# Mixer in the order of the source, scores of two query blocks in two joined PSUM banks, turned five steps behind

## The chip, the core and the metric

The kernel runs on one core of one Trainium2 chip. The metric is the device time of one execution in microseconds; runs of one kernel agree within about 0.05% here (three runs between 880.33 and 881.12). Five engines work side by side: TensorE (PE; matmuls, with PEld for its weight loads), VectorE (DVE), ScalarE (ACT), GpSimd (POOL) and SyncE (SP), whose queue issues most DMA transfers. Each takes its own instructions in the order in which they were built, and waits on semaphores for the others.

## The reference

One layer of an encoder on 512 positions of 1024 features: half a SwiGLU feed-forward network, a mixer, the other half, a final norm.

```python
x = x + 0.5 * swiglu(rms_norm(x, ffn1_norm), ffn1_w_gate, ffn1_w_up, ffn1_w_down)
h = rms_norm(x, mix_norm)
u = h @ w_in                       # 512 Fourier | 8 x 64 q | 2 x 64 k | 2 x 64 v
f_out = fourier_mixer(u[..., :512])            # Re(DFT over positions and channels), a linear map per group
a_out = gqa_attention(q, k, v)                 # norm of q and k, axial rotary, softmax over all 512 keys
x = x + concatenate([f_out, a_out]) @ w_out
x = x + 0.5 * swiglu(rms_norm(x, ffn2_norm), ffn2_w_gate, ffn2_w_up, ffn2_w_down)
return rms_norm(x, final_norm)
```

## The kernel before

The activations lie transposed, features on the 128 partitions and 512 positions along the row: `x` is eight tiles of 128x512. Every product of float32 values is made of three matmuls (`product`, L100): each factor is split into a rounded high part (a cast, by ScalarE in L96 or VectorE in L94) and a low part (`lows`, L72, always VectorE), and high x high, high x low and low x high are added in PSUM. So each weight tile of 128x1024 costs a DMA into a raw tile (`raw_tile`, L85, three buffers, issued by SP), a cast and a `lows` before TensorE can use it. `ring` holds the split weights and the split input `hh`, `hl`; two more slots, `more`, are lent to the mixer.

The program has three stages: FFN1, the mixer, FFN2. The two FFN stages stand in `in_order()`: in them the instructions of TensorE and SP keep the order of the source. The mixer stands outside, so that the framework's scheduler orders all five engines there, by its own estimate of times. VectorE, ScalarE and GpSimd are ordered by that scheduler everywhere. One PSUM pool, `pp` (L51), of eight banks of 128x512 serves all stages; a tile gets a bank when the bank's earlier tile has been read.

The mixer first projects keys (`k`), the first query pair (`q0`) and values (`v`), each 24 matmuls; `rope` rotates keys and queries, and for q1 to q3 moves rows by four small DMAs from `own_q` to `sw_q`, issued by SP (L606). `heads` sums squares per head on TensorE (`pq`, eight columns), and `keys` and `value_stacks` prepare `kst` and `vst`. Four query tiles t = 0 to 3 hold two heads each (b = 0, 1), and each head has four blocks c of 128 queries: 32 steps. In step n `attend(n)` does

- `scores` (L786) of block n: two matmuls of 512 columns into a bank `s`, the negated maximum `mx` over 512 keys on VectorE (L796), its product with the scale (L797), the exponential `e` on ScalarE with its row sum (L799);
- `turn` (L802) of step n - 4: four transposes of `e` into a bank `pt`, a cast to `ph` (ScalarE, L808) and a low part `pl` (VectorE). A turn needs all four blocks of its head;
- `values` (L818) of step n - 6: two matmuls into a bank `o`, and after four of them the sum of its halves into `oo`; after both heads transposes of the row sums (`zp`), a product, and a split into `qa`, `qb`.

Between the steps a list `fill` (L873 to L906) is worked off in proportion: the projections of q1 to q3, then those of the Fourier group (`fproject`, 24 matmuls of 256 columns for a bank `f`, then `fu`, `fe`, `eh`, `el`), the folded map (`fold`), the transforms (`positions`, `dft` and `channels`, `pc`, `psn`, `fq`, `fo`). The raw weights of each come when its `load`, `fload` or `weights` call is made. At last eight `out` tiles (L929) take 24 matmuls each over the eight parts `mh`, `ml` (four Fourier groups, four query tiles), are added to `x`, and feed the norm of FFN2.

## Time and profile before

| | |
|---|---|
| runs | 880.33, 880.73, 881.12 us; median 880.73 |
| the profiled execution | 881.16 us, of which the span of its instructions is 879.4 us |
| granted TensorE clock | 0.996 of full speed |
| FFN1 / mixer / FFN2, by the first k and first gate matmul | to 353.2 us / to 523.5 us / to 879.4 us |
| scores of the 32 steps | 379.2 to 462 us |

A row of the timeline has start, duration, engine, line, operation, output<-inputs, shape and count; in brackets the idle time of the engine before it and what ended that. A matmul's row is longer than the distance to the next start, because matmuls are pipelined. Names of tiles are the program's, without numbers: all `s` banks are `s`. A row of the waits has who waited for whom, the total in us, how often, and the longest.

### The profile page before, as it was taken

To read this page: it belongs to the slowest core of one execution; us is meant where nothing else is said; L and a number is where in the kernel's file an instruction comes from. 1 tells how busy PE (TensorE), PEld (TensorE's weight loads), DVE (VectorE), ACT (ScalarE), POOL (GpSimd) and SP (SyncE) were. 2 spreads that over 40 slices of the span, in tenths; PEclk is the share of its full clock that TensorE was granted. 3 is DMA by queue.
4 is the path that set the end of the run, shared out by engine and by line. 5 is a ranking of instruction groups with operands and counts; after the bars stand their busy time and mean duration, and the time that the engine had idled before them with its cause. 6 is when DMAs were issued, how large, how long until landed. Compare 5 with 4: busy or idle time off the path is not lost.

```text
span 879.4 us, 13481 instructions
## 1 busy us (share of the span) xinstructions
PE 864.5 (98%) x5358; PEld 767.9 (87%) x5358; DVE 641.0 (73%) x1006; ACT 450.4 (51%) x746; POOL 22.9 (3%) x29
## 2 busy tenths in 40 slices
PE   8999999999999999999999999999999999999996
PEld 5888999889989988888888888879998999889986
DVE  7798788459757837699888558977975688459553
ACT  7454466326524635677775446535652366326441
POOL 0000000000000000211000000000000000000001
PEclk9999999999999999999999999999999999999998
DMA  7324232332243113521110213242323232322212
GB/s 247 111 70 164 97 116 85 99 116 105 69 141 114 56 37 108 204 84 37 50 48 25 87 68 133 76 140 98 108 79 129 84 120 82 101 115 86 73 37 96
DMA packets 29151, 85.57 MB, mean 97 GB/s; under 512 B 3488, under 2 KB 6560, under 8 KB 28960
## 3 DMA queue, kind: packets, MB, share of 16 engines
q1 hardware_dynamic: 28560, 83.37, 27.8%
q0 software_dynamic: 384, 1.32, 0.4%
q8 instruction: 42, 0.69, 0.3%
q14 instruction: 21, 0.17, 0.1%
q10 hardware_dynamic: 144, 0.02, 0.0%
HBM read 81.81 MB, written 2.10 MB: 95 GB/s over the span
## 4 chain that ended last, share of the span: by engine, by line
PE 56%; issue 38%; DVE 3%; ACT 2%; DMA 1%; POOL 0%; SPq 0%; DVEq 0%; ACTq 0%; POOLq 0%
PE r L319 10%; PE q L319 5%; PE dn L103 4%; PE dn L102 4%; PE dn L101 4%; PE p L319 3%; PE gu L103 2%; PE gu L102 2%; PE gu L101 2%; PE out L101 2%; PE out L103 2%; PE out L102 2%; PE pt L805 1%; PE q L101 1%; PE q L102 1%
## 5 line engine op out<-in xcount | busy, mean ns | idle before, releaser
L319 PE MATMUL r<-rt,ring 128*128 128x256 f32 x1584 | 207.0, 283 | 0.0
L319 PEld LDWEIGHTS r<-rt,ring 128*128 128x128 f32 x1584 | 196.0, 188 | 2.4
L101 PE MATMUL dn<-at,ring 128*128 128x512 f32 x318 | 125.7, 395 | 0.8 <-ACT ring L96 0.8
L103 PE MATMUL dn<-at,ring 128*128 128x512 f32 x318 | 125.8, 396 | 0.3 <-DVE ring L72 0.3
L102 PE MATMUL dn<-at,ring 128*128 128x512 f32 x318 | 125.6, 395 | 0.0
L405 DVE SCALAR_TENSOR_TENSOR xt<-dn,xt 128x512 f32<-128x512 f32 x61 | 42.1, 689 | 87.4 <-PE dn L103 87.3
L319 PE MATMUL q<-rt,ring 128*128 128x256 f32 x792 | 104.7, 281 | 0.0
L96 ACT CAST ring<-raw_dn 128x768 fp32r<-128x768 f32 (+3 forms) x64 | 48.1, 754 | 107.5 <-PE dn L102 89.1
L319 PEld LDWEIGHTS q<-rt,ring 128*128 128x128 f32 x792 | 98.7, 188 | 0.0
L72 DVE TENSOR_TENSOR ring<-s,ring 128x1024 fp32r<-128x1024 f32 x66 | 80.3, 1220 | 16.9 <-PE r L319 9.7
L280 ACT CAST ring<-s 128x1024 fp32r<-128x1024 f32 x66 | 69.3, 1051 | 37.5 <-PE r L319 19.2
L103 PEld LDWEIGHTS dn<-at,ring 128*128 128x128 f32 x318 | 59.8, 188 | 15.6 <-DVE ring L72 1.5
L101 PEld LDWEIGHTS dn<-at,ring 128*128 128x128 f32 x318 | 59.8, 188 | 14.9 <-ACT ring L96 1.3
L102 PEld LDWEIGHTS dn<-at,ring 128*128 128x128 f32 x318 | 59.8, 188 | 13.7
L72 DVE TENSOR_TENSOR ring<-raw_dn,ring 128x768 fp32r<-128x768 f32 (+3 forms) x64 | 54.5, 854 | 12.0 <-ACT ring L96 9.7
L319 PE MATMUL p<-rt,ring 128*128 128x256 f32 x396 | 52.4, 281 | 0.0
L72 DVE TENSOR_TENSOR ring<-raw_g,ring 128x1024 fp32r<-128x1024 f32 x33 | 40.3, 1223 | 15.4 <-PE p L319 10.9
L319 PEld LDWEIGHTS p<-rt,ring 128*128 128x128 f32 x396 | 49.3, 188 | 0.0
L280 ACT CAST ring<-raw_g 128x1024 fp32r<-128x1024 f32 x33 | 34.6, 1050 | 22.8 <-PE r L319 9.9
L101 PE MATMUL gu<-ring 128*128 128x512 f32 x112 | 44.5, 397 | 0.5 <-ACT ring L542 0.5
L102 PE MATMUL gu<-ring 128*128 128x512 f32 x112 | 44.1, 393 | 0.0
L103 PE MATMUL gu<-ring 128*128 128x512 f32 x104 | 41.0, 394 | 0.7 <-DVE ring L72 0.7
(312 smaller groups left out, 1531.3 us busy)
## 6 DMA issues: line engine op xcount, KB each, us to landing
raw_g<-in_wgu SPq DMA_DIRECT2D x33, 512.0 KB, 3.8
raw_u<-in_wgu SPq DMA_DIRECT2D x33, 512.0 KB, 4.2
raw_dn<-in_wd SPq DMA_DIRECT2D x40, 384.0 KB, 3.1
raw_gu<-in_wgu SPq DMA_DIRECT2D x16, 512.0 KB, 3.6
raw_o<-in_wo SPq DMA_DIRECT2D x8, 512.0 KB, 3.5
raw_in<-in_wins SPq DMA_DIRECT2D x6, 512.0 KB, 4.0
raw_dn<-in_wd SPq DMA_DIRECT2D x8, 320.0 KB, 2.9
raw_dn<-in_wd SPq DMA_DIRECT2D x8, 256.0 KB, 2.6
```

Source lines behind the costliest of these rows:

```text
L72: nc.vector.tensor_tensor(out=lo, in0=src, in1=asf(hi), op=ALU.subtract)
L96: nc.scalar.copy(hi[:, :n, :], raw[:, :n, :])
L101: nc.tensor.matmul(ps, whi, mhi, start=first, stop=False)
L102: nc.tensor.matmul(ps, whi, mlo, start=False, stop=False)
L103: nc.tensor.matmul(ps, wlo, mhi, start=False, stop=last)
L280: nc.scalar.copy(hi, src)
L319: nc.tensor.matmul(ps, a[:, ks], b[:, i], start=first and i == 0 and o == 0, stop=i == KH - 1 and o == 2, skip_group_check=not first,)
L405: nc.vector.scalar_tensor_tensor(out=x[d][:, t], in0=ps[:, t], scalar=0.5, in1=x[d][:, t], op0=ALU.mult, op1=ALU.add)
L805: nc.tensor.transpose(pt[:, c * P : (c + 1) * P], prob[t, b, c][:, kc * P : (kc + 1) * P], ident)
```

## The change

The mixer moves into `in_order()`, so TensorE's and SP's instructions keep the source's order there too. PSUM is no longer one pool: FFN1 has a pool of eight banks, the mixer one of six and a tile `st` of two joined banks, FFN2 again eight. `scores` now does two blocks at a time, in even steps: four matmuls into the halves of `st`, one maximum over both (128x2 from 128x2x512), one product, two exponentials. `st` is one tile, so each pair writes where the pair before stood. `turn` comes five steps after a step's number instead of four, `values` seven instead of six, and the loop has 39 steps.

The DMA for raw weights is separated from their split: `fetch` issues it at places written into the source, and `project` and `fload` take the raw tile. cos and sin come after the third weight tile. Some calls move by a few matmuls (`key_scales` after seven parts of q0 instead of five, `keys` after all of `v`, `value_stacks` after part five of q1). `out` sums its parts in the order 0, 1, 2, 4, 5, 6, 3, 7. Of all instructions only the maxima and their products change in number, from 32 each to 16.

In the built program two more waits stand: the first k matmul waits for VectorE's residual of FFN1's last `dn` bank, and the first gate matmul of FFN2 for the residual of the last `out` bank.

```diff
-    pp = ctx.enter_context(tc.tile_pool(name="psum", bufs=8, space=bass.MemoryType.PSUM))
+    pools = []
+
+    def banks_in(name, n):
+        return tc.tile_pool(name=name, bufs=n, space=bass.MemoryType.PSUM)

     def bank(name):
-        return pp.tile([P, S], F32, tag="bank", name=name)
+        return pools[-1].tile([P, S], F32, tag="bank", name=name)
...
-    with in_order():
+    with in_order(), banks_in("psum1", 8) as psum:
+        pools.append(psum)
+        warm()
         ffn(n0, n1, A["wgu1"], A["wd1"], A["wdt1"], GROUPS1, opening1, None)
...
-    with tc.tile_pool(name="mix", bufs=1) as mp, tc.tile_pool(name="mixt", bufs=1) as mt:
+    with (
+        in_order(),
+        tc.tile_pool(name="mix", bufs=1) as mp,
+        tc.tile_pool(name="mixt", bufs=1) as mt,
+        banks_in("psum2", 6) as psum,
+        banks_in("psum3", 1) as two,
+    ):
+        pools.append(psum)
...
+        st = two.tile([P, 2, S], F32, name="st")
+
+        def scores(t, b, c0):
+
+            if b == 0 and c0 == 0:
                 zs[t] = tp.tile([P, 4, 2], F32, tag="z", bufs=2, name=f"z{t}")
             q = (qa, qb)[b][t]
-            cs = slice(c * P, (c + 1) * P)
-            ps = bank(f"s{t}{b}{c}")
-            nc.tensor.matmul(ps, q[:, cs], kst[b][0], start=True, stop=False)
-            nc.tensor.matmul(ps, q[:, cs], kst[b][1], start=False, stop=True)
-            f = sc[:, c, 2 + 2 * t + b : 3 + 2 * t + b]
-            mx = tp.tile([P, 1], F32, tag="mx", bufs=8, name=f"mx{t}{b}{c}")
-            nc.vector.tensor_reduce(out=mx, in_=ps, axis=AX.X, op=ALU.max, negate=True)
-            nc.vector.tensor_tensor(out=mx, in0=mx, in1=f, op=ALU.mult)
-            e = temp(f"e{t}{b}{c}")
-            nc.scalar.activation(e, ps, AF.Exp, bias=mx, scale=f, accum_out=zs[t][:, c, b : b + 1])
-            prob[t, b, c] = e
+            both = range(c0, c0 + 2)
+            for c in both:
+                cs = slice(c * P, (c + 1) * P)
+                nc.tensor.matmul(st[:, c - c0], q[:, cs], kst[b][0], start=True, stop=False)
+                nc.tensor.matmul(st[:, c - c0], q[:, cs], kst[b][1], start=False, stop=True)
+            i = 2 + 2 * t + b
+            mx = tp.tile([P, 2], F32, tag="mx", bufs=4, name=f"mx{t}{b}{c0}")
+            nc.vector.tensor_reduce(out=mx, in_=st, axis=AX.X, op=ALU.max, negate=True)
+            nc.vector.tensor_tensor(out=mx, in0=mx, in1=sc[:, c0 : c0 + 2, i], op=ALU.mult)
+            for c in both:
+                e = temp(f"e{t}{b}{c}")
+                o = c - c0
+                nc.scalar.activation(
+                    e, st[:, o], AF.Exp, bias=mx[:, o : o + 1], scale=sc[:, c, i : i + 1],
+                    accum_out=zs[t][:, c, b : b + 1],
+                )
+                prob[t, b, c] = e
...
+        fetch(0)
+        fetch(1)
         key = project(0, "k")
         q0 = project(1, "q0")
+        fetch(5)
+        nc.sync.dma_start(out=cos, in_=A["cos"])
+        nc.sync.dma_start(out=sin, in_=A["sin"])
         run(key)
         rope("k", qkg[:, 1:2])
         n1.column([n1.acc])
+        fetch(2)
         val = project(5, "v")
-        run(q0[:5])
+        run(q0[:7])
         key_scales()
-        run(q0[5:])
+        run(q0[7:])
...
+                if k == 2:
+                    add(fetch, (4, "f0", "f1")[t - 1])
                 if t == 3 and k in (0, 4):
                     add(fload, k // 4)
-                if k == 3:
+                if t == 3 and k == 6:
+                    add(fetch, "f2")
+                if k == 5 if t == 1 else k == 3:
...
-            if n < 32:
+            if 5 <= n < 37:
+                turn(*at(n - 5))
+            if n < 32 and n % 2 == 0:
                 scores(*at(n))
-            if 4 <= n < 36:
-                turn(*at(n - 4))
-            if n >= 6:
-                values(*at(n - 6))
+            if n >= 7:
+                values(*at(n - 7))
...
+        ready = 0, 1, 2, 4, 5, 6, 3, 7
         for d in range(KD):
             whi, wlo = weights(A["wo"][d], f"o{d}")
             ps = bank(f"out{d}")
-            for k in range(KD):
-                product(ps, whi[:, k, :], wlo[:, k, :], mh[k], ml[k], k == 0, k == KD - 1)
+            for k in ready:
+                product(ps, whi[:, k, :], wlo[:, k, :], mh[k], ml[k], k == ready[0], k == ready[-1])
...
-    with in_order():
+    with in_order(), banks_in("psum4", 8) as psum:
+        pools.append(psum)
          ffn(n2, n3, A["wgu2"], A["wd2"], A["wdt2"], GROUPS2, lambda gate, column, row: [[gate(0, {KD - 1: column}), gate(1, {3: row})]], closing)
```

More of the change, by code (lines that the diff above doesn't have):

```diff
@@ L506, in encoder, with warm @@
     nc.vector.memset(idle, 0.0)
-    busy = bank("busy")
-    for _ in range(WARM):
-        nc.tensor.matmul(busy, idle[:, 0:P], idle, start=True, stop=True)
+    def warm():
+        busy = bank("busy")
+        for _ in range(WARM):
+            nc.tensor.matmul(busy, idle[:, 0:P], idle, start=True, stop=True)
     n0, n1 = Norm(0), Norm(1)
@@ L571, in encoder @@
         cos = mp.tile([P, S], F32, name="cos")
-        nc.sync.dma_start(out=cos, in_=A["cos"])
         sin = mp.tile([P, S], F32, name="sin")
-        nc.sync.dma_start(out=sin, in_=A["sin"])
         chan = mp.tile([P, 4, P], F32R, name="chan")
@@ L579, in encoder, with fetch @@
         sc = mp.tile([P, 4, 10], F32, name="sc")
+        raws = {}
+        def fetch(c):
+            if isinstance(c, int):
+                raws[c] = raw_tile(A["wins"][c], f"in{c}")
+            elif c == "fw":
+                raws[c] = raw_tile(A["fw"].rearrange("p (a b) -> p a b", b=P), c, 4)
+            else:
+                raws[c] = raw_tile(A["winf"][int(c[1])].rearrange("p a (b c) -> p (a b) c", c=P), c)
         def project(c, name):
-            whi, wlo = weights(A["wins"][c], f"in{c}")
+            whi, wlo = weights(None, f"in{c}", raw=raws[c])
             ps = bank(name)
@@ L694, in fload @@
             if i == "fw":
-                fws[i] = [
-                    w[:, :4, :].rearrange("p a b -> p (a b)")
-                    for w in weights(A["fw"].rearrange("p (a b) -> p a b", b=P), "fw", 4)
-                ]
+                fws[i] = [w[:, :4, :].rearrange("p a b -> p (a b)") for w in weights(None, i, 4, raws[i])]
                 return
-            src = A["winf"][i].rearrange("p a (b c) -> p (a b) c", c=P)
-            if i == 3 and i not in fws:
-                fws[i] = raw_tile(src, "f3")
-                return
-            h, l = weights(src, f"f{i}", raw=fws.get(i))
+            h, l = weights(None, f"f{i}", raw=raws[f"f{i}"])
             fws[i] = [w.rearrange("p (a b) c -> p a (b c)", a=4) for w in (h, l)]
@@ L784, in encoder @@
         prob, parts, outs, pair, zs = {}, {}, {}, {}, {}
-        def scores(t, b, c):
-            if b == 0 and c == 0:
+        st = two.tile([P, 2, S], F32, name="st")
+        def scores(t, b, c0):
+            if b == 0 and c0 == 0:
                 zs[t] = tp.tile([P, 4, 2], F32, tag="z", bufs=2, name=f"z{t}")
             q = (qa, qb)[b][t]
-            cs = slice(c * P, (c + 1) * P)
-            ps = bank(f"s{t}{b}{c}")
-            nc.tensor.matmul(ps, q[:, cs], kst[b][0], start=True, stop=False)
-            nc.tensor.matmul(ps, q[:, cs], kst[b][1], start=False, stop=True)
-            f = sc[:, c, 2 + 2 * t + b : 3 + 2 * t + b]
-            mx = tp.tile([P, 1], F32, tag="mx", bufs=8, name=f"mx{t}{b}{c}")
-            nc.vector.tensor_reduce(out=mx, in_=ps, axis=AX.X, op=ALU.max, negate=True)
-            nc.vector.tensor_tensor(out=mx, in0=mx, in1=f, op=ALU.mult)
-            e = temp(f"e{t}{b}{c}")
-            nc.scalar.activation(e, ps, AF.Exp, bias=mx, scale=f, accum_out=zs[t][:, c, b : b + 1])
-            prob[t, b, c] = e
+            both = range(c0, c0 + 2)
[15 more added lines that the diff above has]
+                prob[t, b, c] = e
         def turn(t, b, kc):
@@ L857, in encoder @@
             nc.gpsimd.dma_start(out=t, in_=A[n])
+        fetch(3)
         q1 = project(2, "q1")
-        run(val[:2])
+        run(val)
         keys()
-        run(val[2:5])
         heads("q0", 1, scale)
-        run(val[5:])
         scaled_values()
@@ L893, in encoder @@
                         add(fload, 3)
+                        add(fetch, "fw")
                 if h == 0 and n == 0:
                     add(heads, "q3", 4, scale)
-                if h == 0 and n in (1, 2):
-                    add(fload, n + 1)
+                    add(fetch, "f3")
+                if h == 0 and n == 1:
+                    add(fload, 2)
                 if h == 1 and n == 0:
@@ L910, in at @@
                 return m // 8, m // 4 % 2, m % 4
-            if n < 32:
+            if 5 <= n < 37:
+                turn(*at(n - 5))
+            if n < 32 and n % 2 == 0:
                 scores(*at(n))
-            if 4 <= n < 36:
-                turn(*at(n - 4))
-            if n >= 6:
-                values(*at(n - 6))
+            if n >= 7:
+                values(*at(n - 7))
         whole = sum(c for c, _, _ in fill)
         done = 0.0
-        for n in range(38):
-            while fill and done < whole * (FILL_LEAD + (1 - FILL_LEAD) * n / 38):
+        for n in range(39):
+            while fill and done < whole * (FILL_LEAD + (1 - FILL_LEAD) * n / 39):
                 done += fill[0][0]
```

## The prediction

> **What bounds the kernel now.** I read the page first, then the stretches of the mixer, then who TensorE waited for in it.

> ```profile
> span 879.4 us, 13481 instructions
> PE 864.5 (98%) x5358; PEld 767.9 (87%) x5358; DVE 641.0 (73%) x1006; ACT 450.4 (51%) x746; POOL 22.9 (3%) x29
> ```

> TensorE is the bound, 98% busy; the rest of the span is all that better order can win, 14.9 us, and the change touches only the mixer, from 353 us (the first k matmul) to 523.5. The stretches, columns PE, PEld, DVE, ACT, POOL (busy us and instructions), granted clock, DMA share, GB/s:

> ```profile
> 379.00:392.00 13.00, 13.00 (x68) 10.79 (x67) 12.40 (x29) 9.54 (x20) 3.28 (x2) 1.00 0.20 63
> 392.00:402.00 10.00, 10.00 (x58) 8.41 (x56) 9.73 (x21) 7.79 (x16) 0.11 (x1) 1.00 0.30 74
> 402.00:412.00 10.00, 8.76 (x62) 7.75 (x62) 9.51 (x24) 7.95 (x18) 2.36 (x3) 1.00 0.17 56
> ...
> 432.00:442.00 10.00, 9.10 (x67) 8.17 (x66) 7.60 (x17) 6.51 (x15) 0.00 (x0) 1.00 0.13 50
> ...
> 462.00:472.00 10.00, 9.14 (x64) 7.65 (x63) 8.64 (x20) 6.73 (x17) 0.62 (x1) 1.00 0.13 52
> sum 173.00, PE 169.51 PEld 144.18 DVE 133.82 ACT 109.59 POOL 14.57; mean PE 12.11 PEld 10.30 DVE 9.56 ACT 7.83 POOL 1.04
> ```

> TensorE is idle for 173.00 - 169.51 = 3.5 us in the mixer. VectorE has no room just where the scores begin: 12.40 of 13, 9.73 of 10, 9.51 of 10.

> ```profile
> PE o L824 <- ACT ph L808: 1.4, 2, 0.9
> PE f L715 <- ACT e L799: 1.2, 1, 1.2
> PE s L792 <- ACT e L799: 0.5, 1, 0.5
> PE pt L805 <- ACT e L799: 0.4, 1, 0.4
> ```

> All five waits are for ScalarE's exponentials (e) or casts (ph). Each costs more than its idle time: a matmul's row is 0.17 us longer than the way to the next start (0.40 against 0.23, below), and the second matmul after a stop starts 0.22 after the first, not 0.12 (1.42 for twelve, below):

> ```profile
> 403.98 0.39 PE L715 MATMUL f<-ring 128*128 128x256 f32 x1 [1.24 <-ACT e L799]
> 404.20 0.28 PE L716 MATMUL f<-ring 128*128 128x256 f32 x1
> ```

> With 0.1 to 0.27 more for each of five, 3.5 us become at most 4.6, the most that can be won; I take 4.6.

> **The two pool edges.** The built order shows a new wait. PSUM pools now end with their stage, so the first k matmul waits for VectorE's residual on FFN1's last bank, and the first gate matmul of FFN2 for that of the last `out` bank. Before, neither waited:

> ```profile
> 352.95 0.40 PE L103 MATMUL dn<-at,ring 128*128 128x512 f32 x1
> 353.19 0.39 PE L101 MATMUL k<-ring 128*128 128x512 f32 x1
> ...
> 353.39 0.69 DVE L405 SCALAR_TENSOR_TENSOR xt<-dn,xt 128x512 f32<-128x512 f32 x1 [0.86 <-PE dn L103]
> ...
> 523.30 0.39 PE L103 MATMUL out<-qa,ring 128*128 128x512 f32 x1
> 523.53 0.39 PE L101 MATMUL gu<-ring 128*128 128x512 f32 x1
> ...
> 523.73 0.69 DVE L934 TENSOR_TENSOR xt<-out,xt 128x512 f32<-128x512 f32 x1 [2.76 <-PE out L103]
> ```

> The residual ends at 354.08, so k starts 0.9 us late, 1.0 with the restart; at 523.53 the same, 1.0. VectorE idles ahead of both, nothing hides them. All of TensorE queues behind. Together +2.0 us (1.8 without restarts).

> **The joined scores.** Sixteen maxima over 128x1024 replace 32 over 128x512, and 16 small products go. A 512 maximum takes 0.60 us to the next start, a 1024-wide operation 1.14:

> ```profile
> 402.51 0.68 DVE L796 TENSOR_REDUCE mx<-s 128x1 f32<-128x512 f32 x1
> 403.11 0.68 DVE L614 TENSOR_TENSOR sw_q<-sw_q,sin 128x512 f32<-128x512 f32 x1
> ...
> 390.91 1.23 DVE L72 TENSOR_TENSOR ring<-raw_f,ring 128x1024 fp32r<-128x1024 f32 x1
> 392.05 0.15 DVE L797 TENSOR_TENSOR mx<-mx,sc 128x1 f32<-128x1 f32 x1
> ```

> No 1024-wide maximum is in the trace; bounds are 1.14 (that row) and 1.20 (two maxima); I take 1.14, as the form of cost is the same. VectorE saves 16 x 0.06 = 1.0 us and 16 products of up to 0.15 (the last row), in all 1 to 3 us, not on TensorE's path by itself. [...]

> What costs is that `st` exists once. Its next four matmuls wait for the second exponential of the pair before; the 32 old banks had no such wait. The loop without queueing, from these rows:

> ```profile
> 382.23 0.40 PE L792 MATMUL s<-ks,qa 128*128 128x512 f32 x1
> 382.47 0.39 PE L793 MATMUL s<-ks,qa 128*128 128x512 f32 x1
> ...
> 384.38 0.78 ACT L799 ACTIVATE e<-s,mx,sc 128x512 f32<-128x512 f32 x1 [1.72 <-DVE mx L797]
> 385.15 0.77 ACT L799 ACTIVATE e<-s,mx,sc 128x512 f32<-128x512 f32 x1
> ...
> 396.50 0.60 PE L805 MATMUL pt<-ident,e 128*128 128x128 f32 x4
> 396.86 0.48 PE L825 MATMUL o<-pl,vst 128*128 128x512 f32 x1
> ```

> Three starts 0.23 apart and an end, 1.1; maximum 1.2; product 0.15; exponentials 0.77 + 0.78; handovers 0.1: 4.1 us. TensorE's own work from one pair to the next, with projection matmuls in the fill: four scores 0.95, four value matmuls 0.95, two sets of transposes 0.36 each, nine projection matmuls 2.1, sums of squares now and then 0.8, so 4.7 to 5.5. With Fourier matmuls in it, 24 of 256 columns at 1.42 the dozen:

> ```profile
> 96.00 1.42 PE r L319 x12
> ```

> 0.95 + 0.95 + 0.72 + 2.85 = 5.5. So a pair stalls TensorE as soon as its maximum, product and exponentials together queue more than about 1 us (early) or 1.4 us (later) behind other work, on two engines that take their instructions strictly in the built order.

> I walk that order with the durations of the rows, on a clock shifted by the first edge's 1.03.

> **Pair 2.** The values' transposes stand two matmuls later in q1 than before:

> ```profile
> 376.93 0.60 PE L681 MATMUL vp<-ident,vt 128*128 128x128 f32 x4
> ```

> 376.93 + 1.03 + 0.46 + 0.36 and three matmuls at 0.25: the first pair starts at 379.5, and q1, with three matmuls behind the pair, ends at 381.3. ScalarE's next entries are the square and `own` of q1, then the table load, then the exponentials:

> ```profile
> 380.03 0.60 ACT L598 ACTIVATE sq_q<-q 128x512 f32<-128x512 f32 x1
> 380.66 0.69 ACT L602 ACTIVATE own_q<-q,qkg 128x512 f32<-128x512 f32 x1
> 381.37 1.28 ACT L799 ACT_TABLE_LOAD   x1
> ```

> 381.3 + 0.6 + 0.7 + 1.3 + 0.8 + 0.8 = 385.5. TensorE has only twelve matmuls to do and stands from 383.25: 2.25 us.

> **Pair 3.** Its scores wait for pair 2's exponentials. Pair 2 starts at 385.55, its matmuls end at 386.75, the maximum at 387.9, then the rope product on the swapped q1 (0.6) stands ahead of the small product, 388.65; exponentials end 390.3. TensorE has four scores, nine matmuls and one set of sums, to 389.55: 0.75.

> **Pair 4.** On VectorE the next maximum stands behind f0's cast and low part (1.14) and a query's low part:

> ```profile
> 387.95 0.69 DVE L94 CAST ring<-raw_f 128x1024 fp32r<-128x1024 f32 x1
> 388.68 0.69 DVE L72 TENSOR_TENSOR qa<-rot_q,qa 64x512 fp32r<-64x512 f32 x1
> ```

> From 388.65: rope sum and two small operations 0.85, cast 0.6, low part 1.15, wait and qa 0.8, maximum 1.15, qb 0.6, two small ones 0.25: 394.05. ScalarE is at q2's square and `own` until 394.5, so both exponentials end at 396.1; TensorE (four scores, nine matmuls, two sets of transposes) is there at 394.2: 1.9.

> **Pairs 5 to 10.** The same walk gives 0.8 (maximum behind a cast's and a pl's wait), 0.45 and 1.1 (ScalarE's cast of f2, the square and `own` of q3 ahead of the exponentials); from pair 8, when the projections are through, TensorE's 5.5 us cover the loop to within 0.15.

> **Pairs 11 to 16.** Pair 11 waits 2.6: f3's low part stands ahead of the maximum, and two pl and an oo at 0.6 each between it and its product. Pair 14 waits 2.55: two fe, two pl and a qb keep the maximum back 1.35, an el and a pl its product 1.2:

> ```profile
> L726 DVE SCALAR_TENSOR_TENSOR fe<-f,r,fu 128x256 f32<-128x256 f32 x8 | 3.5, 476 | 0.6 <-PE f L717 0.6
> ```

> Pair 16 waits 1.9: o0's low part ahead of the maximum, a pl and two fe ahead of the product, a map cast and an eh ahead of the exponentials. The others find their pair done.

> With restarts: 2.35 + 0.85 + 2.0 + 0.9 + 0.55 + 1.2 = 7.85 up to pair 7, then 0.25 + 2.7 + 2.65 + 2.0 = 7.6. Bounds: nothing, if every pair is served at once, and 15 x 1.5 = 22, if every pair stalls like the mean of the ten that do. I take the walk, nearer the upper end, since it puts no operation ahead of another that the built order doesn't.

> **The lead and the order of SP.** Turning five steps on takes the waits on e and ph away: -4.6. Six banks for the rest bring no wait over 0.2 in the walk. SP now issues the raw fetches between the swaps of q1 to q3; f0 stands behind q1's four swaps:

> ```profile
> 381.38 2.48 SPq L606 DMA_DIRECT2D sw_q<-own_q  x4
> raw_f<-in_winf SPq DMA_DIRECT2D x4, 512.0 KB, 3.5
> ```

> `own` ends near 382.7, f0 lands at 382.7 + 2.5 + 0.5 + 3.5 = 389.2, needed 389.5: hidden by 0.3 us of VectorE's other work; f1 by about as little. Late, each costs up to 1 us on a saturated VectorE. cos, sin and the raw weights of q1 to q3 only change places with a neighbour in SP's queue: nothing, or up to 1 us if k's rope finds cos late. The new order of k in `out` (the third Fourier group, then the heads, then the fourth) leaves 0.4 us at the third group's cast, in the walk; 0 to 2. Moving the v matmuls, key scales and value stacks keeps their number and, by the walk, meets no wait; each transposes or sums a few columns, 0.4 to 0.8 us, and would show as a gap if late.

> **Sum.** 2.0 + 7.85 + 7.6 + 0.4 - 4.6 = +13.25; the walk's own clock, which rounds less, ends 12.1 later. I take 12: the profiled run 881.16 (span 879.4 and 1.76 around it) becomes 893.2. The median is 0.43 below that run: 892.7.

> **The rivals.**
> A. The join costs nothing: the loop of 4.1 fits under 5.1 at every pair. For it: VectorE gets 1 to 3 us of room, and TensorE 1.0 to 1.4 us of slack a pair. Against: 12.40 of 13, and the casts and low parts ahead of the maxima in the built order. It decides where the queues' delay stays below 1 us a pair. Time: -4.6 + 2.0 + 2.35 (the table load of pair 2) = 880.5 at the median; without that stall too, 878.1. Not slower.
> B. Only the saturated head stalls: the later pairs, with VectorE at 7.6 to 8.6 of 10, are served in time. -4.6 + 2.0 + 7.85 + 0.4 = +5.65: 886.4.
> C. Stalls beget late transfers: f0, f1 and the `out` weights come late as well, 3 to 4 us more: 896.

> **Chances.** Forecast 0.56, B 0.20, C 0.09, A 0.15. A measurement tells 0.2%, 1.8 us, from no change; A splits 0.10 faster, 0.05 same, and the others are slower, 0.85. The range leaves out A and little of C: 884 to 897, which holds the forecast's own 889 to 896 and B.

> **What would show it.** Right: the first k and gate matmuls 0.9 us after the `dn` and `out` end, released by VectorE; TensorE's `st` matmuls waiting for e in at least eight of 15 pairs, the first over 2 us; VectorE's idle share up between 383 and 415; about 16 us of TensorE idle in the mixer. Wrong: `st` matmuls that find e done; idle below 6 us; a maximum far from 1.2 us; gaps at `pt` or `o` instead.

## The result, and the profile after

The changed kernel takes 899.26 us in the median of five runs (897.63 to 900.84), against 880.73 (880.33 to 881.14): ratio 1.0212, 95% interval 1.0201 to 1.0223, slower by 18.5 us where 12.0 were forecast. The time lies above the range, which ended at 897. Line numbers above the mixer are three higher than before: the scores' matmuls are L812 and L813, the maximum L816, its product L817, the exponential L821, the residual L408.

The page of the changed kernel, its profiled run being the one of 900.84 us, the slowest of the five; the last row shown is the granted clock in 40 slices:

```profile
span 899.1 us, 13464 instructions
...
PE 872.0 (97%) x5358; PEld 780.3 (87%) x5358; DVE 639.8 (71%) x974; ACT 451.1 (50%) x746; POOL 24.5 (3%) x29
...
PEclk9999999999999999979999999999999999999997
```

TensorE's busy time did not stay at 864.5 us; it grew by 7.5 with the same 5358 matmuls, and one slice of the mixer shows 7 where there were only nines. The stretches of the mixer, columns as before, show where:

```profile
379.00:392.00 13.00, 10.17 (x35) 8.15 (x34) 8.05 (x18) 7.29 (x14) 3.05 (x2) 0.74 0.20 61
392.00:402.00 10.00, 8.15 (x35) 6.46 (x35) 7.12 (x12) 3.87 (x8) 1.19 (x1) 0.83 0.34 110
...
442.00:452.00 10.00, 9.39 (x53) 8.46 (x54) 4.93 (x8) 4.92 (x11) 0.00 (x0) 0.83 0.16 54
...
462.00:472.00 10.00, 9.53 (x54) 8.76 (x55) 4.26 (x6) 5.00 (x11) 0.00 (x0) 0.83 0.00 1
```

The granted clock, 1.00 in all of these stretches before, is 0.74 and three times 0.83. VectorE, which had no room between 379 and 402 (12.40 of 13, 9.73 of 10), now has plenty (8.05 and 7.12). TensorE's waits, in us in total, times, longest:

```profile
PE st L812 <- ACT e L821: 13.4, 8, 2.8
...
PE k L104 <- DVE xt L408: 0.9, 1, 0.9
PE gu L104 <- ACT ring L99: 0.9, 1, 0.9
```

The waits for `ph` and the turns' waits for `e` are gone, and the scores wait for the exponentials of the pair before. In the timeline these are the first matmuls of pairs 2, 4, 5, 6, 7, 11, 14 and 16, and the two edges of the stage:

```profile
352.10 0.47 PE L104 MATMUL k<-ring 128*128 128x512 f32 x1 [0.88 <-DVE xt L408]
...
384.44 0.50 PE L812 MATMUL st<-ks,qa 128*128 128x512 f32 x1 [2.83 <-ACT e L821]
...
397.49 0.50 PE L812 MATMUL st<-ks,qb 128*128 128x512 f32 x1 [1.85 <-ACT e L821]
...
404.31 0.50 PE L812 MATMUL st<-ks,qa 128*128 128x512 f32 x1 [0.61 <-ACT e L821]
...
411.14 0.50 PE L812 MATMUL st<-ks,qa 128*128 128x512 f32 x1 [0.89 <-ACT e L821]
...
417.17 0.50 PE L812 MATMUL st<-ks,qb 128*128 128x512 f32 x1 [0.87 <-ACT e L821]
...
442.61 0.57 PE L812 MATMUL st<-ks,qb 128*128 128x512 f32 x1 [2.42 <-ACT e L821]
...
444.25 0.63 PE L849 MATMUL o<-ph,vst 128*128 128x512 f32 x1
444.68 0.63 PE L850 MATMUL o<-pl,vst 128*128 128x512 f32 x1
...
462.47 0.50 PE L812 MATMUL st<-ks,qa 128*128 128x512 f32 x1 [2.29 <-ACT e L821]
...
477.00 0.50 PE L812 MATMUL st<-ks,qb 128*128 128x512 f32 x1 [1.60 <-ACT e L821]
...
543.37 0.47 PE L104 MATMUL gu<-ring 128*128 128x512 f32 x1 [0.88 <-ACT ring L99]
```

Two value matmuls behind pair 11's stall, at 444.25 and 444.68, start 0.43 us apart; a matmul of 512 columns starts 0.23 after the one ahead at full clock. They run at half clock.

The clock's record in the trace changes only at multiples of 3.413 us from one another. Here is TensorE in single steps of that raster (columns as above; the first number after the comma is TensorE's busy time, the third number from the end its clock):

```profile
381.46:384.88 3.42, 0.59 (x3) 0.40 (x3) 0.76 (x2) 2.91 (x5) 0.00 (x0) 1.00 0.31 75
384.88:388.29 3.41, 3.41 (x13) 2.83 (x11) 1.89 (x3) 0.10 (x1) 0.00 (x0) 0.50 0.44 156
388.29:391.71 3.42, 3.42 (x11) 2.84 (x11) 2.70 (x6) 2.72 (x6) 1.12 (x1) 0.50 0.00 0
395.12:398.53 3.41, 1.56 (x10) 1.14 (x8) 1.70 (x3) 2.77 (x7) 0.00 (x0) 1.00 0.20 48
398.53:401.94 3.41, 3.41 (x12) 2.75 (x11) 2.69 (x5) 0.00 (x0) 0.00 (x0) 0.50 0.77 267
...
473.62:477.04 3.42, 1.82 (x11) 1.30 (x9) 3.42 (x7) 3.23 (x9) 0.00 (x0) 1.00 0.37 122
477.04:480.45 3.41, 3.41 (x22) 3.02 (x22) 3.02 (x4) 2.98 (x5) 0.00 (x0) 1.00 0.28 111
```

A step in which TensorE works for 0.59 or 1.56 us is followed by half clock, one with 1.82 is not. Five steps in the mixer are at half clock, the others behind pairs 11 and 14.

The two traces give this ledger for the mixer. "Start to start" is the distance between the starts of two matmuls less its usual length in the trace of before.

| us, start to start | before | after |
|---|---|---|
| k to the first gate matmul | 170.3 | 191.3, and 1.0 ahead of k |
| the two edges | 0 | 2.1 |
| waits of scores, `out` and one scale | 0.7 (one wait) | 16.6 |
| waits at `pt`, `o`, `f` | 3.9 | 0 |
| matmuls at half clock | 0 | 7.6 |

So 2.1 + 16.6 + 7.6 - 4.6 = 21.7 of the mixer's 22.0 are named. The span grew by 19.7 only; the FFN stages, which no edit but the edges touches, were together 2.2 us shorter in this run than in the profiled run of before. When the clock first becomes full is not the reason: that was 6.2 us into the span of before and 9.4 here (4.2 to 10.7 in the traces of this study). The FFN's matmuls themselves have other distances: those of `dn` (512 columns) start 0.228 us apart here and 0.233 before, those of `p` (256 columns) 0.120 here and 0.119 before. All six traces of kernels with a joined tile show the first pair of numbers, and all seven without it the second (0.232 to 0.233 and 0.119). Over the two stages this is a gain of an estimated 2 to 3 us for the kernels with a joined tile, worked out from these distances and from the stages' lengths. What in a joined tile of the mixer does this to the FFN is open.

### The profile page after: what moved, and what is told of

It is laid out like the page before. It is cut to its first block, busy times and chain, and to the rows that moved or that the text cites. A ratio compares the mean times of both kernels' runs of the same rounds, so it can differ in the third digit from the quotient of the medians.

```text
span 899.1 us, 13464 instructions
## 1 busy us (share of the span) xinstructions
PE 872.0 (97%) x5358; PEld 780.3 (87%) x5358; DVE 639.8 (71%) x974; ACT 451.1 (50%) x746; POOL 24.5 (3%) x29
## 4 chain that ended last, share of the span: by engine, by line
PE 89%; ACT 4%; DVE 3%; DMA 2%; issue 1%; POOL 0%; SPq 0%; POOLq 0%; ACTq 0%; DVEq 0%
PE r L322 21%; PE q L322 11%; PE dn L106 8%; PE dn L104 8%; PE dn L105 8%; PE p L322 5%; PE gu L104 4%; PE gu L106 4%; PE gu L105 4%; PE out L105 2%; PE out L106 2%; PE out L104 2%; ACT e L821 1%; PE pt L830 1%; PE st L812 1%
## 5 line engine op out<-in xcount | busy, mean ns | idle before, releaser
L322 PEld LDWEIGHTS r<-rt,ring 128*128 128x128 f32 x1584 | 198.0, 192 | 1.9
L104 PE MATMUL dn<-at,ring 128*128 128x512 f32 x318 | 124.0, 390 | 0.8 <-ACT ring L99 0.8
L106 PE MATMUL dn<-at,ring 128*128 128x512 f32 x318 | 124.1, 390 | 0.6 <-DVE ring L75 0.6
L105 PE MATMUL dn<-at,ring 128*128 128x512 f32 x318 | 124.0, 390 | 0.0
L408 DVE SCALAR_TENSOR_TENSOR xt<-dn,xt 128x512 f32<-128x512 f32 x61 | 42.0, 690 | 82.2 <-PE dn L106 82.2
## 6 DMA issues: line engine op xcount, KB each, us to landing
raw_g<-in_wgu SPq DMA_DIRECT2D x33, 512.0 KB, 3.8
raw_u<-in_wgu SPq DMA_DIRECT2D x33, 512.0 KB, 4.3
raw_gu<-in_wgu SPq DMA_DIRECT2D x16, 512.0 KB, 3.5
raw_o<-in_wo SPq DMA_DIRECT2D x8, 512.0 KB, 3.5
raw_in<-in_wins SPq DMA_DIRECT2D x6, 512.0 KB, 6.6
```

The lines of the kernel that those rows point to most:

```text
L104: nc.tensor.matmul(ps, whi, mhi, start=first, stop=False)
L105: nc.tensor.matmul(ps, whi, mlo, start=False, stop=False)
L106: nc.tensor.matmul(ps, wlo, mhi, start=False, stop=last)
L322: nc.tensor.matmul(ps, a[:, ks], b[:, i], start=first and i == 0 and o == 0, stop=i == KH - 1 and o == 2, skip_group_check=not first,)
L408: nc.vector.scalar_tensor_tensor(out=x[d][:, t], in0=ps[:, t], scalar=0.5, in1=x[d][:, t], op0=ALU.mult, op1=ALU.add)
```

## The experiments

**Keep TensorE at work through five stalls.** All filler runs have these lines, with other numbers; they add nothing to the sums.

```diff
+    zero = cp.tile([P, S], BF16, name="zero")
+    nc.vector.memset(zero, 0.0)
+    FILLER = {2: 10, 6: 6, 20: 8, 26: 8, 30: 5}
...
+            if n in FILLER:
+                t, b, _ = at(n - 7)
+                ps = banks["q2"] if n == 2 else banks["q3"] if n == 6 else outs[t, b]
+                for _ in range(FILLER[n]):
+                    nc.tensor.matmul(ps, zero[:, 0:P], zero, start=False, stop=False)
             if n < 32 and n % 2 == 0:
                 scores(*at(n))
```

> The changed kernel with 37 more matmuls that add zeros (bfloat16, 128x512) into a bank that is being summed anyway, placed ahead of the scores of pairs 2, 4, 11, 14 and 16, 10, 6, 8, 8 and 5 of them, so that TensorE works where it stood 2.83, 1.85, 2.42, 2.29 and 1.60 us. Theory: the stalls are paid twice, once as waiting (about 16.5 us in the mixer) and once as half clock in the 3.41 us after a long one (matmuls at 0.427 us instead of 0.232, 7.6 us in the profiled run). With TensorE kept at work the waits for e end when they did, so only the second part goes: granted clock 0.995 or more, 1.00 in every stretch of the mixer, 5 to 8 us less than the changed kernel, 891.5 to 894.5. Rival: the slow matmuls come from the change itself (joined banks, the sums of two columns) and not from the standing still: clock stays at 0.986 to 0.990 and the time does not fall, or rises by what the extra matmuls add.

897.91 us (897.38 to 901.26), ratio 1.0197 [1.0174, 1.0220], clock 0.992; the theory's 891.5 to 894.5 was missed. Inconclusive for the time: but for the clearing of `zero` only TensorE's instructions were edited, yet the scheduler, which estimates times, then put ScalarE's and VectorE's instructions of the head in another order, and a new wait arose at pair 6:

```profile
412.13 0.80 PE L815 MATMUL st<-ks,qa 128*128 128x512 f32 x1 [4.09 <-ACT e L824]
```

Half clock followed this wait, and only this one: behind the five filled places the clock stayed full. In the next two runs the other engines keep the changed kernel's order, but for the clearing and one entry each on ScalarE and VectorE.

**Four stalls filled, in the changed kernel's order.**

```diff
-    FILLER = {2: 10, 6: 6, 20: 8, 26: 8, 30: 5}
+    FILLER = {2: 7, 6: 6, 20: 8, 26: 8}
```

> The changed kernel with zeros added by 7, 6, 8 and 8 more matmuls ahead of the scores of pairs 2, 4, 11 and 14, so chosen that VectorE and ScalarE keep the changed kernel's order but for one pair of neighbours near the mixer's end; in the first filler run they did not, and the waits moved. Theory: the waits end when they did in the changed kernel, and no stretch of 3.41 us after them runs at half clock. Of the 7.6 us, 2.7 (behind pairs 11 and 14) come back whole, and of the head's part only what pairs 3 and 5 do not then wait instead, 1.5 to 3: 893.5 to 895.5, granted clock 0.994 or more. Rival 1: the slow matmuls do not come from standing still: the clock stays at 0.986 to 0.990, time 898 or more. Rival 2: in the head VectorE and ScalarE set the end, and all the half clock there was hidden: 896 to 897.

893.79 us (893.07 to 894.79), ratio 1.0142 [1.0128, 1.0156], clock 0.996 and 0.997 in every run. Stretches and the place of pair 2:

```profile
379.00:392.00 13.00, 11.45 (x54) 8.32 (x55) 9.36 (x18) 8.10 (x16) 4.02 (x2) 1.00 0.21 61
392.00:402.00 10.00, 8.77 (x46) 6.46 (x45) 8.13 (x15) 6.95 (x15) 1.47 (x1) 1.00 0.40 133
```

```profile
381.58 1.46 PE L957 MATMUL q<-zero 128*128 128x512 bf16 x6
383.79 0.50 PE L815 MATMUL st<-ks,qa 128*128 128x512 f32 x1 [0.75 <-ACT e L824]
...
388.71 0.50 PE L815 MATMUL st<-ks,qb 128*128 128x512 f32 x1 [0.73 <-ACT e L824]
```

(Six of the seven matmuls put in here have a row.) Scores start no earlier than the exponentials allow, so the stalls are paid as before; but the clock is 1.00 everywhere, and 5.5 us are gone (899.26 to 893.79; by the ratios 0.0070 x 881 = 6.2). The slow matmuls come from standing still. Less than 7.6 comes back, in part because pair 3, which found its tile free while TensorE was slow, now waits 0.73. What is left above the kernel before is 12.5 us, near the forecast's 12.0, but partly by luck: in the traces the mixer with its first edge is 14.5 us longer than before, and the FFN stages are 2.6 shorter.

**The two late stalls filled.**

```diff
-    FILLER = {2: 10, 6: 6, 20: 8, 26: 8, 30: 5}
+    FILLER = {20: 8, 26: 8}
```

> The same with the fillers of pairs 11 and 14 alone, 8 matmuls each. Theory: the head keeps its half clock (379 to 402), the two later stretches of half clock go, each 1.2 to 1.5 us: 896 to 897.5. Rival: those stretches are hidden behind the next pair's wait: within 0.8 us of the changed kernel.

897.20 us (894.02 to 898.51), ratio 1.0178 [1.0164, 1.0193]: 2.1 us less by the medians, 3.0 by the ratios, as expected. Its profiled run, of 894.02, shows one thing that makes the runs differ. Pair 4's wait was 1.91 us long, as in the changed kernel (1.85), but lay across a border of the raster, 0.7 us on one side and 1.2 on the other, and no half clock followed. Pair 2's stall was followed by one step at half clock in place of two. At about 1.5 us a step, two steps fewer would be the 3 us by which this run lies below its median.

**Each block's scores in a bank of its own.** The join alone is undone, with the pairs' order on TensorE kept:

```diff
-            for c in both:
-                nc.tensor.matmul(st[:, c - c0], q[:, cs], kst[b][0], start=True, stop=False)
...
-            nc.vector.tensor_reduce(out=mx, in_=st, axis=AX.X, op=ALU.max, negate=True)
+            pss = {c: bank(f"s{t}{b}{c}") for c in both}
...
+            for c in both:
...
+                nc.vector.tensor_reduce(out=mx, in_=pss[c], axis=AX.X, op=ALU.max, negate=True)
...
-        banks_in("psum2", 6) as psum,
-        banks_in("psum3", 1) as two,
+        banks_in("psum2", 8) as psum,
```

> The changed kernel with the join alone undone: each block's scores in a bank of its own out of eight, a maximum, a product and an exponential for each; TensorE's and SP's written order, the later turn, the pools by stage stay. Theory: the one joined tile is what TensorE waits for; without it no scores wait for e, both pool edges stay (0.9 us each), the turn five steps on takes most of the 4.6 us of waits of the kernel before away, clock 0.995 or more: 878 to 883. Rival: the written order and VectorE's queue stall TensorE with or without the join (transposes that wait for e, value matmuls for ph or pl): 886 or more, with over 8 us of waits in the mixer.

882.69 us (881.40 to 884.08), ratio 1.0018 [1.0008, 1.0027], clock 0.996: the joined tile carries 16.6 of the 18.5 us. VectorE and ScalarE do the maxima and exponentials in smaller parts, and TensorE waits for them once, for a maximum:

```profile
PE s L810 <- DVE mx L816: 0.4, 1, 0.4
```

Undoing the join here also gives the scores a share of eight banks in place of two; a run below separates the two. And as the kernels with a joined tile have the shorter FFN stages, the tile costs the mixer more than the difference of the times, by the 2 to 3 us estimated above.

**The same, with one pool for the whole kernel.**

```diff
-    pools = []
+    pools = [ctx.enter_context(tc.tile_pool(name="psum", bufs=8, space=bass.MemoryType.PSUM))]
...
-    with in_order(), banks_in("psum1", 8) as psum:
-        pools.append(psum)
+    with in_order():
```

> The kernel of the run with the join undone, and the eight banks in one pool for the whole kernel, as before the change. Theory: the two edges cost 1.0 each: k and the first gate matmul start 0.23 us after the matmul ahead of them, and the time is 2.0 us (1.6 to 2.4) under that run. Rival: something else holds k and the gate back next (k's weights, VectorE's norm): less than 1 us gained.

880.87 us (879.41 to 883.47), ratio 0.9999 [0.9988, 1.0010]; the kernel before spread from 880.13 to 883.08 over 19 runs beside it, so less than about 1 us is not told here. The edges are worth 1.8 us together. The written order, the later turn and the moved fetches are worth nothing in sum: without the join the waits that they took away are replaced by others of about the same size, of which the three longest in the mixer of this run are

```profile
PE dft L101 <- DVE ring L72: 0.9, 1, 0.9
...
PE out L102 <- DVE el L72: 0.6, 1, 0.6
PE kp L674 <- DVE kw L668: 0.5, 1, 0.5
```

The wait at `kp` is one that the first edge had covered: there k came 0.9 us later, and `kw` was done.

**The joined tile twice**, with four banks for the rest:

```diff
+            st = two.tile([P, 2, S], F32, tag="st", name=f"st{t}{b}{c0}")
...
-        banks_in("psum2", 6) as psum,
-        banks_in("psum3", 1) as two,
+        banks_in("psum2", 4) as psum,
+        banks_in("psum3", 2) as two,
```

> The changed kernel with the joined tile twice (four banks), and four banks for all the rest. Theory: that there is one such tile is the cause, not its width: with two, the scores of a pair wait for the exponentials of the pair before the last, which the walk has done in time except at pair 3 or 4; under 4 us of waits at st, clock 0.993 or more, 880 to 887, the upper part if four banks make pt, o or q wait for a bank. Rival: the 1024-wide maximum and the pair's exponentials in a row are late in any case, or four banks are too few: 890 or more, with the waits at st, pt or o.

891.28 us (889.35 to 893.49), ratio 1.0115 [1.0093, 1.0137]: above the theory's 887, and where the rival put it (890 or more, waits at `o` and `pt`). No score waits any more, but value matmuls do, 4.6 us for the low part `pl`, and 13.7 us run at half clock. In VectorE's timeline the longest of these waits ends with the row of 428.37:

```profile
426.09 1.23 DVE L815 TENSOR_REDUCE mx<-st 128x2 f32<-128x1024 f32 x1 [1.95 <-PE st L812]
427.23 1.22 DVE L75 TENSOR_TENSOR ring<-raw_f,ring 128x1024 fp32r<-128x1024 f32 x1
428.37 0.68 DVE L75 TENSOR_TENSOR pl<-pt,ph 128x512 fp32r<-128x512 f32 x1
```

VectorE stood 1.95 us for the pair's scores, then did the wide maximum and a weight's low part, and `pl`, whose `ph` was done at 426.4, came last. A second tile takes the wait from the scores; the maximum of a pair, in a queue taken strictly in order, holds up what stands behind it. Turns wait 1.2 us for a `pl` that frees their bank, so the four banks for the rest have a part in it, which was not tried apart.

**Two banks for scores, not joined.**

```diff
-            pss = {c: bank(f"s{t}{b}{c}") for c in both}
+            pss = {c: two.tile([P, S], F32, tag="s", name=f"s{t}{b}{c}") for c in both}
...
-        banks_in("psum2", 8) as psum,
+        banks_in("psum2", 6) as psum,
+        banks_in("psum3", 2) as two,
```

> The changed kernel with each block's scores, maximum, product and exponential apart, but in two banks set aside for scores, beside six for the rest: the places of the joined tile without the join. A pair's first block waits for the first exponential of the pair before, its second block for the second. Theory A: it is the small number of banks for scores that stalls; the join adds that the first exponential stands behind both blocks' maximum, and the first scores behind the second exponential, 0.6 + 0.8 = 1.4 us a pair where TensorE waits: half or more of the loss stays, 888 to 894, scores that wait for e. Theory B: without the join the ends of the exponentials are early enough for two banks: 882 to 886, close to the run with eight banks (882.7). Rival: VectorE's 32 smaller maxima make it as late as the join does: 897 or more.

894.51 us (893.65 to 895.34), ratio 1.0150 [1.0135, 1.0165]; half a microsecond above theory A's range. The scores wait for the exponentials, and 10.2 us run at half clock:

```profile
PE s L811 <- ACT e L819: 6.0, 6, 1.7
```

No other wait inside the mixer is longer than 0.6 us, so the six banks for the rest are enough. Of the 16.6 us that the joined tile carries 11.8 come with two banks for scores in place of a share of eight, and 4.8 with the join itself. These are differences of medians from three series (11.6 and 5.5 by the ratios), and the join's part is net of its shorter FFN stages.

**The join alone, in the scheduler's order**, made from the kernel before: `scores` and the pools as in the change, called in even steps.

```diff
-            if n < 32:
+            if n < 32 and n % 2 == 0:
                 scores(*at(n))
```

> The kernel before with the join alone: two banks joined in a pool of their own beside six, one maximum for a pair, the pools by stage; TensorE and SP in the planner's order, turned four steps on. Theory: the one joined tile costs what it costs in any order, since the way from its scores to its second exponential is 4.1 us or more on VectorE and ScalarE while the other banks would let TensorE go on: 890 or more, scores that wait for e, half clock after the long ones. Rival: the planner sets other work between the pairs, so that the tile is free in time, and it was the written order that made it late: 880 to 886.

907.85 us (906.47 to 910.15), ratio 1.0303 [1.0288, 1.0319], 26.6 us more than before: the theory's time, but not its waits. The scores wait 1.3 us in six short waits; the scheduler let other work go first, and the turns and values are late instead:

```profile
PE pt L827 <- ACT e L818: 11.2, 6, 3.9
PE o L846 <- ACT ph L830: 5.6, 8, 2.4
```

The written order with the later turn, worth nothing without the join, saves 8.6 us with it.

**What a stall costs by itself**, in the FFN of the kernel before:

```diff
+                def late(j, t, ps):
+                    z = sp.tile([P, HALF], BF16, tag="late", name=f"late{n_}_{j}")
+                    nc.gpsimd.tensor_copy(z, t)
+                    for _ in range(2 * (j % LATE)):
+                        nc.gpsimd.tensor_copy(z, z)
+                    nc.tensor.matmul(ps, zero, z, start=False, stop=False, skip_group_check=True)
...
                     elif n == 4:
+                        late(j, b["p5"], b["r"])
                         multiply(b["r"], "s2", "t2", w, False)
```

> The kernel before with one wait of TensorE put into each of the FFN's products in seven (before the fifth of them): GpSimd copies a small tile 1, 3, 5 or 7 times, and a matmul that adds zeros waits for it; nothing else waits for those copies. This measures what a stall costs by itself, in a part where TensorE is otherwise 100% busy at full clock. Theory: short stalls (1 us) cost themselves and 0.2 to 0.3 us; those that fill more than about half of a 3.41 us stretch between two possible changes of the clock put the next 3.41 us at half clock, 1.4 to 1.7 us on top; which of two equal stalls does depends on how it lies to that raster. Rival: the half clock needs TensorE to stand a whole such stretch, or comes from the mixer's small matmuls: no half clock here after stalls under 3.4 us.

1035.3 us in one run, clock 0.943, 112.6 us at half clock ahead of the kernel's end. The stalls came out at up to 5.9 us. Steps of the clock's raster around three of them:

```profile
225.74:229.16 3.42, 1.01 (x5) 1.01 (x5) 0.23 (x1) 0.00 (x0) 2.11 (x5) 0.50 0.43 175
229.16:232.57 3.41, 3.41 (x17) 3.41 (x17) 0.59 (x1) 1.32 (x2) 0.00 (x0) 0.50 0.00 0
703.61:707.02 3.41, 1.64 (x14) 1.54 (x14) 3.38 (x7) 1.36 (x3) 1.18 (x2) 1.00 0.68 237
707.02:710.44 3.42, 0.23 (x3) 0.23 (x3) 2.10 (x3) 1.05 (x1) 2.95 (x4) 1.00 0.48 186
...
850.38:853.80 3.42, 1.67 (x15) 1.56 (x14) 1.66 (x4) 1.27 (x3) 0.98 (x2) 1.00 0.51 153
853.80:857.21 3.41, 1.20 (x11) 1.20 (x11) 1.40 (x2) 0.30 (x1) 1.97 (x4) 1.00 0.00 0
857.21:860.62 3.41, 3.41 (x19) 3.41 (x18) 0.96 (x1) 0.91 (x2) 0.00 (x0) 0.50 0.25 51
```

All steps of that run between 15 and 1020 us in which TensorE's brackets of idle time fill at least 0.3 of the step, or which are at half clock, sorted by that share:

| the step's clock | idle share of the step | steps | clock of the next step |
|---|---|---|---|
| full | 0.31 to 0.52 | 18 | full in all |
| full | 0.60 to 1.00 | 21 | half in all |
| half | 0.00 to 0.22 | 21 | full in all |
| half | 0.24 to 0.70 | 12 | half in all |

This separates without one exception, and it decides for the theory: no whole idle step was needed, and no matmuls of the mixer. (The step of 1024 us, at the kernel's end, is left out: it has 0.30 idle and is followed by half clock, as the last section tells.) The run took 154.0 us longer than the kernel before. TensorE's waits for the late tiles are 104.3 us of these; the other 49.7 are 1.5 us for each of the 33 steps at half clock, restarts included.

**The waits left without the join.** Two runs tried to beat the kernel before, from the version with one pool.

```diff
-        keys()
         heads("q0", 1, scale)
+        keys()
...
-        add(fold, cost=1.3)
...
+                if h == 1 and n == 2:
+                    add(fold, cost=1.3)
...
-        ready = 0, 1, 2, 4, 5, 6, 3, 7
+        ready = 0, 1, 4, 5, 6, 2, 3, 7
```

> The kernel with the join undone and one pool (880.87 against 880.93 of the kernel before), with its three remaining longer waits moved: the third Fourier group's product in `out` after the heads' (0.62 us for its el), the key's transposes behind q0's sums (0.52 us for kw), the map's product one group earlier (0.94 us for the bank whose map low part was late). Theory: nothing else waits there, 1.5 to 2 us less: 878.8 to 879.5, faster than both by more than 0.1%. Rival: the waits only move to the next operand: within 0.8 us of 880.9.

880.44 us (877.82 to 883.32), ratio 0.9989 [0.9977, 1.0001]. The folded map overwrites two tiles of the split input that the last Fourier projections still read, so in this version these are computed from other numbers; the instructions are the same in kind and number. Two of the three waits went, and the key's side came back as 1.0 us at the first scores, for `ks`. The order in `out` was then moved alone:

```diff
-        ready = 0, 1, 2, 4, 5, 6, 3, 7
+        ready = 0, 1, 4, 5, 6, 2, 3, 7
```

> The kernel with the join undone and one pool, with one thing moved: in `out` the third Fourier group's product comes after the first three heads'. Every other engine keeps its order. Theory: the 0.62 us that TensorE waited there for el go and nothing takes their place: 0.6 to 0.8 us less than the run with one pool, 880.0 to 880.4, about the kernel before. Rival: the next head's low part (qb) is as late as el was: no gain, 880.9.

881.18 us (879.32 to 882.76), ratio 0.9999 [0.9990, 1.0009]. The 0.6 us at `out` are gone from the waits, but `kp` waited 0.9 us in this profile instead of 0.5. Neither version is surely faster than the kernel before.

## Why the prediction was wrong in size

**The edges** were right: 0.88 us idle at k and at the first gate matmul, 1.0 each from start to start, 1.8 in the runs with and without them. At the gate matmul the profile names a weight's cast that ended 0.1 us after the residual; the same cast stands beside running gate matmuls in the run with one pool, so it is not what they wait for.

**The walk of the joined scores** was right in place and nearly in size. Start to start, forecast and measured:

| pair | 2 | 3 | 4 | 5 | 6 | 7 | 8 to 10 | 11 | 14 | 16 | `out` |
|---|---|---|---|---|---|---|---|---|---|---|---|
| forecast | 2.35 | 0.85 | 2.0 | 0.9 | 0.55 | 1.2 | 0.25 | 2.7 | 2.65 | 2.0 | 0.4 |
| measured | 2.99 | 0 | 2.10 | 0.85 | 1.13 | 1.12 | 0.47 | 2.66 | 2.53 | 1.85 | 0.50 |

With 0.37 at the very first pair, for a scale, that is 16.6 against 15.85. The sum is closer than its terms, and that is luck: pair 3, forecast 0.85, did not wait, because TensorE was slow ahead of it at half clock, and pairs 2 and 6 were 0.6 longer each. The order that the walk gave for pair 11 stands so in VectorE's timeline, the weight's low part ahead of the maximum, two `pl` and an `oo` between it and its product:

```profile
436.68 1.22 DVE L75 TENSOR_TENSOR ring<-raw_f,ring 128x1024 fp32r<-128x1024 f32 x1 [1.78 <-ACT ring L99]
437.82 1.22 DVE L816 TENSOR_REDUCE mx<-st 128x2 f32<-128x1024 f32 x1
438.95 0.68 DVE L75 TENSOR_TENSOR pl<-pt,ph 128x512 fp32r<-128x512 f32 x1
439.55 0.67 DVE L857 TENSOR_TENSOR oo<-o,oo 64x512 f32<-64x512 f32 x1
440.15 0.67 DVE L75 TENSOR_TENSOR pl<-pt,ph 128x512 fp32r<-128x512 f32 x1
440.74 0.14 DVE L817 TENSOR_TENSOR mx<-mx,sc 128x2 f32<-128x2 f32 x1
```

The maximum starts 1.13 us ahead of the next operation; 1.14 was taken. So joining two maxima of 0.60 saves VectorE 0.07 us (1.20 less 1.13), where the rows of before gave 0.06. All four signs listed as right were there: k and gate 0.9 late, 8 waits at `st` of which the first is over 2 us, VectorE idler between 383 and 415, and 13.4 us of scores' idle time plus 2.3 at the edges, `out` and the first pair.

**The step that failed** is the price of a stall: "Each costs more than its idle time", by 0.1 to 0.27 us for the restart. That was read from five waits of before, the longest 1.24 us, in stretches whose granted clock was 1.00 throughout. The change makes five stalls longer than all of those, and the four of 1.85 to 2.83 us each put the next step of the clock's raster, or two, at half clock: 7.6 us that no term of the sum held, 5.5 to 6.2 net as the filled stalls show, of the 6.5 us by which the forecast fell short. The term "With restarts" was mis-sized by that; the mechanism it was added to was right. Smaller, and not told apart from the spread of the runs: 12 was taken, after the walk's own clock, where the list of terms gave 13.25. In the profiled run the mixer and the edges missed by 9.7 us in all (21.7 against 12: 7.6 at half clock, 1.25 of that choice, 0.85 of the walk and the edges). That only 6.5 show in the time is because the FFN stages came out 2.2 us shorter, which the forecast held at nothing, and because the profiled run is the slowest of its five.

The clock's record in the trace of the changed kernel shows steps of 3.413 us, or a whole number of them, between changes, and 0.50 as the only lower clock. No whole idle step went ahead of the slow ones: at pair 4, 1.85 us within one step were enough.

**The removed waits**, -4.6, are gone from the changed kernel as forecast, and from the run with each block's scores in its own bank too, where no stalls at the scores cover them. But they are no gain that could be kept by undoing the join: with one pool and the scores apart, other waits take their place and the time is that of before.

**The rivals.** A fell: the loop of 4.1 us is not what decides, the queues ahead of its parts are. B fell: pairs 11, 14 and 16 stall for 7.0 us. C, the closest number, 896, had another mechanism: the first Fourier weights were not late, VectorE's cast of f0 has no wait ahead of it, and no later cast of a raw weight in the mixer waits for a DMA.

```profile
389.74 0.69 DVE L97 CAST ring<-raw_f 128x1024 fp32r<-128x1024 f32 x1
```

## What to carry to other kernels

A joined operation saves its engine a little and makes a whole pair one link of a chain: count how many tiles the waiting engine may fill ahead, for two banks for scores cost 11.8 us here and the join 4.8 more, against 16 x 0.07 = 1.1 us saved on VectorE. When stalls of TensorE are priced, add to each that may fill half of one 3.413 us step of its clock's raster (0.54 was enough here, 0.47 was not) the matmuls that then run at half speed, about 1.5 us a step (49.7 us over the 33 slow steps of the run with stalls). And an edit of one engine's instructions can reorder the others where a scheduler places them: compare the built orders before a difference is put down to the edit.
